# Products of constants in the waits that a kernel's own planner foresees for TensorE

## The chip, the core and the metric

The kernel runs on one core of a Trainium2 chip. The metric is the device time of one execution in microseconds (us), the median of three runs: 2536.06 us for the kernel before (2533.53 to 2548.08). Smaller is better.

## What is computed

One layer of a decoder trunk on 2048 tokens of width 1024, in fp32. The reference, cut to its frame:

```python
h = rms_norm(x, mix_norm_g)
qa, ka, va, pb, qm = split_cols(h @ w_in, ...)          # one combined projection
out_a = sliding_window_attention(q, k, va, sinks, rel_bias)      # 6 heads, window 128
out_b = rwkv7_mixer(token_shift(pb, mu), ...)           # 6 heads, a recurrent scan
out_m = memory_attention(qm, mk, mv)                    # 4 heads, 256 memory tokens
x = x + concat([out_a, out_b, out_m]) @ w_out
x = x + conv_ffn(rms_norm(x, ffn_norm_g), w_up, conv_w, conv_b, w_down)   # d_ff 2816
```

## The kernel before

The kernel is recorded first and written out afterwards. Each call on an engine goes into a `Recorder`, which notes an operation with its tiles, a duration from the function `cost` (L374) and what it depends on. `Recorder.order` (L229) and `run` (L257) then lay all operations out on a modelled time axis, engine by engine: when an engine is free, the ready operation with the longest modelled path behind it starts. Each operation `o` thereby has a modelled `o.start` and `o.end`. `Recorder.emit` (L330) writes the real instructions in that order; semaphores for the dependencies are added behind it. Beyond setting the order, the modelled times are used for nothing. All instructions are written by one line of `emit`, L345, so every row of the profile has L345, and groups are told apart by their tiles.

The work in order of time, by the profile:

- 0 to some 960 us: the input projection (tile `mm`: 4 blocks of 512 tokens x 17 column groups, each 8 x 3 products of 512 columns, since each fp32 operand is split into a high and a low fp32r part) with its post-processing (`st`, `bc`, `tpv`: transposes by the constant identity `ident`, a part of the tile `cst`), the RWKV scan (`pz`, `pc`, `pg`, `p1`, `px`, `pq`, `pu`, `pS`), and from 435 us on the window attention (`pl`, `tpa`, `po`) and the memory attention (`plm`, `tpm`, `pm`).
- to 1236 us: the output projection (`outproj`, L1271), four blocks of 512 tokens, the first two beside attention and scan. At the end of each block come the sums of squares of the new x: `st2` (the profile writes `st`), four fp32 products of a 128x128 tile `ss` with one column of ones, each into one column of a PSUM tile. From them follow `s` (VectorE), `r` (GpSimd), `tpr` (a TensorE transpose), `rt` (ScalarE), and the DMA to `drs`, on SyncE's queue.
- to the end: the feed-forward network in seven products for eight (`seven`, L1380; tiles `uf`, `uch`, `uip`), first `ffn_up` for both halves of the tokens, then `ffn_down`. It takes weights from DMA (`wraw`), split by ScalarE (`whi`) and VectorE (`wlo`).

PSUM is held in rings: tag `mm` has one buffer (used by `mm`, by `st2` and by `tpr`), so has `po`; `f`, `ch` and `ip` have two. A new tile of a ring waits until the last reader of the tile that held the buffer is done. A product with `start=True` overwrites what its PSUM tile held.

Of the kernel before, what the change touches and what calls it, by code (L numbers as in the profile page):

```python
# [18 lines left out]
P = 128  # L19
# [34 lines left out]
class View:  # L54
# [42 lines left out]
    def real(self):  # L97
        r = self.t.made()
        for f, a, k in self.path:
            r = bass.AP(r.tensor, r.offset + a[0], a[1]) if f == "ap" else getattr(r, f)(*a, **k)  # L100
        return r
# [28 lines left out]
class Recorder:  # L130
# [126 lines left out]
    def run(self):  # L257
# [69 lines left out]
        assert len(out) == len(ops)  # L327
        return out

    def emit(self, tc):  # L330
        nc, open_ = tc.nc, {}
        real = lambda v: v.real() if isinstance(v, View) else v
        out = self.out = self.order()
        with tc.manual_schedule():
            for o in out:
                if o.eng is None:
                    p = o.a[0]
                    if o.fn == "open":
                        kw = {k: v for k, v in (("space", p.space), ("side", p.side)) if v is not None}
                        open_[p] = tc.tile_pool(name=p.name, bufs=p.bufs, reuse_waits="tile", **kw)  # L340
                        p.obj = open_[p].__enter__()
                    else:
                        open_.pop(p).__exit__(None, None, None)
                else:
                    getattr(getattr(nc, o.eng), o.fn)(*map(real, o.a), **{k: real(v) for k, v in o.k.items()})  # L345
        return open_

# [59 lines left out]
class K:  # L407
# [5 lines left out]
    def consts(self):  # L413
        nc, tc, a = self.nc, self.tc, self.a
        p = self.rec.pool("const", 1)
        self.cp = p
        c = p.tile([P, CSTW], F32, name="cst")
        nc.sync.dma_start(out=c[:, 0:P], in_=a["cst"][:, 0:P])
        nc.sync.dma_start(out=c[:, P:], in_=a["cst"][:, P:])
        self.c = {n: c[:, o:o + w] for n, (o, w) in CST.items()}  # L420
        pp = p.tile([P, PPW], F32, name="pp")
        nc.sync.dma_start(out=pp, in_=a["pp"])
        self.pp = {n: pp[:, o:o + w] for n, (o, w) in PPC.items()}
        self.ident = self.c["ident"]
        self.mh = self.cp.tile([P, 10], F32, name="mh")
        nc.vector.memset(self.mh, -0.5)
        self.one = self.cp.tile([P, 1], F32, name="one")
        nc.vector.memset(self.one, 1.0)
# [1272 lines left out]
```

## Time and profile before

| | before |
|---|---|
| median of 3 runs | 2536.06 us (2533.53 to 2548.08) |
| the profiled execution | 2532.01 us |
| its span | 2530.1 us |
| mean granted TensorE clock | 0.966 of full |
| TensorE (PE) busy | 2403.9 us, 95% of the span |
| VectorE (DVE) busy | 2037.7 us, 81% |
| ScalarE (ACT) busy | 1256.3 us, 50% |
| DMA engines, mean busy share | 49.1% of 16 engines' span on the main queue |

The span is the time from the first to the last instruction; 1.9 us of the profiled execution lie around it. PE stands for the products on TensorE and PEld for its weight loads, which overlap the product before. A plain fp32 product is carried out as two passes, each with a weight load of its own: it stands in the program once and in the profile twice. Products of fp32r operands and transposes are one pass. In the profile's rows, `128*64 128x384` means a stationary operand of 128 rows and 64 columns and a moving operand of 384 columns. "Granted clock" 1.00 is 2.4 GHz, 0.50 is 1.2 GHz.

### The profile page before, as it was taken

To read this page: it belongs to the slowest core of one execution; us is meant where nothing else is said; L and a number is where in the kernel's file an instruction comes from. 1 tells how busy PE (TensorE), PEld (TensorE's weight loads), DVE (VectorE), ACT (ScalarE), POOL (GpSimd) and SP (SyncE) were. 2 spreads that over 40 slices of the span, in tenths; PEclk is the share of its full clock that TensorE was granted. 3 is DMA by queue.
4 is the path that set the end of the run, shared out by engine and by line. 5 is a ranking of instruction groups with operands and counts; after the bars stand their busy time and mean duration, and the time that the engine had idled before them with its cause. 6 is when DMAs were issued, how large, how long until landed. Compare 5 with 4: busy or idle time off the path is not lost.

```text
span 2530.1 us, 36859 instructions
## 1 busy us (share of the span) xinstructions
PE 2403.9 (95%) x12268; PEld 1897.1 (75%) x12268; DVE 2037.7 (81%) x4901; ACT 1256.3 (50%) x2541; POOL 78.5 (3%) x53
## 2 busy tenths in 40 slices
PE   8898999899898989999899999999999998999999
PEld 6777777666676757667788788888888886887887
DVE  6677778778778777769688998899888888878876
ACT  5354544555445554555354455565545463444442
POOL 1111011010000010000000000000000000000000
PEclk9999999989989989999999999999999998999999
DMA  7675745744344464547323733353233256548543
GB/s 230 192 214 153 212 131 149 203 138 121 114 134 124 128 183 137 177 134 259 109 97 111 265 130 106 111 179 137 99 108 106 88 166 205 166 150 274 157 146 111
DMA packets 292935, 389.32 MB, mean 154 GB/s; under 512 B 49911, under 2 KB 155392, under 8 KB 292744
## 3 DMA queue, kind: packets, MB, share of 16 engines
q1 hardware_dynamic: 292744, 386.96, 49.1%
q8 instruction: 97, 1.59, 0.3%
q14 instruction: 94, 0.77, 0.1%
HBM read 274.89 MB, written 111.97 MB: 153 GB/s over the span
## 4 chain that ended last, share of the span: by engine, by line
PE 77%; DVE 9%; DMA 6%; issue 4%; ACT 3%; SPq 0%; POOL 0%; POOLq 0%; DVEq 0%; ACTq 0%
PE uf L345 27%; PE mm L345 15%; PE uch L345 13%; PE uip L345 6%; PE pq L345 4%; DMA nb<-nbd 3%; PE pg L345 2%; PE po L345 2%; DMA wraw<-w_ip_in 2%; DVE wlo L345 1%; DVE uc L345 1%; PE pl L345 1%; PE tpa L345 1%; DVE h2l L345 1%; PE pu L345 1%
## 5 line engine op out<-in xcount | busy, mean ns | idle before, releaser
L345 ACT CAST whi<-wraw 128x512 fp32r<-128x512 f32 (+1 forms) x410 | 250.3, 613 | 367.8 <-PE mm L345 135.2
L345 PE MATMUL uf<-h2h,wlo 128*128 128x512 f32 x1056 | 412.4, 392 | 14.1 <-DVE wlo L345 14.1
L345 PE MATMUL uf<-h2h,whi 128*128 128x512 f32 x1056 | 413.9, 392 | 8.5 <-ACT whi L345 6.0
L345 PE MATMUL uf<-h2l,whi 128*128 128x512 f32 x1056 | 413.0, 391 | 0.0
L345 DVE TENSOR_TENSOR wlo<-wraw,whi 128x512 fp32r<-128x512 f32 (+1 forms) x410 | 277.3, 679 | 101.5 <-ACT whi L345 99.6
L345 ACT CAST whi<-ws 128x512 fp32r<-128x512 f32 (+1 forms) x272 | 164.8, 609 | 348.8 <-PE uf L345 163.7
L345 DVE SCALAR_TENSOR_TENSOR uc<-ub,pp,uc 128x1024 f32<-128x1024 f32 x176 | 225.0, 1282 | 26.2 <-ACT uc L345 25.2
L345 PE MATMUL mm<-hh,whi 128*128 128x512 f32 x544 | 226.7, 418 | 18.6 <-ACT whi L345 6.6
L345 PEld LDWEIGHTS uf<-h2h,wlo 128*128 128x128 f32 x1056 | 199.6, 189 | 57.0 <-DVE wlo L345 15.1
L345 PEld LDWEIGHTS uf<-h2h,whi 128*128 128x128 f32 x1056 | 199.4, 189 | 53.9 <-ACT whi L345 8.1
L345 PEld LDWEIGHTS uf<-h2l,whi 128*128 128x128 f32 x1056 | 199.6, 189 | 41.7 <-DVE h2l L345 0.7
L345 PE MATMUL mm<-hh,wlo 128*128 128x512 f32 x544 | 221.9, 409 | 1.4 <-DVE wlo L345 1.4
L345 PE MATMUL mm<-hl,whi 128*128 128x512 f32 x544 | 223.0, 410 | 0.0
L345 PE MATMUL uch<-h2h,whi 128*128 128x512 f32 x528 | 205.7, 390 | 0.1
L345 PE MATMUL uch<-h2h,wlo 128*128 128x512 f32 x528 | 205.8, 390 | 0.0
L345 PE MATMUL uch<-h2l,whi 128*128 128x512 f32 x528 | 205.5, 389 | 0.0
L345 DVE TENSOR_TENSOR wlo<-ws,whi 128x512 fp32r<-128x512 f32 (+1 forms) x272 | 181.3, 672 | 23.3 <-ACT whi L345 22.0
L345 PEld LDWEIGHTS mm<-hh,whi 128*128 128x128 f32 x544 | 105.9, 195 | 47.1 <-ACT whi L345 8.8
L345 ACT CAST h2h<-tr 128x512 fp32r<-128x512 f32 x182 | 110.3, 620 | 58.5 <-DMA tr<-dg 35.4
L345 DVE TENSOR_TENSOR xtmp<-xinv,nb 96x60 f32<-96x60 f32 (+24 forms) x496 | 100.7, 203 | 38.7 <-DMA nb<-nbd 34.5
L345 DVE TENSOR_TENSOR h2l<-tr,h2h 128x512 fp32r<-128x512 f32 x182 | 120.3, 688 | 9.2 <-ACT h2h L345 9.1
L345 ACT ACTIVATE uc<-ub,pp 128x1024 f32<-128x1024 f32 x88 | 109.7, 1247 | 34.0 <-DVE ub L345 32.9
(366 smaller groups left out, 4721.5 us busy)
## 6 DMA issues: line engine op xcount, KB each, us to landing
wraw<-w_up_in SPq DMA_DIRECT2D x176, 256.0 KB
tr<-dg SPq DMA_DIRECT2D x154, 256.0 KB
wraw<-w_ip_in SPq DMA_DIRECT2D x136, 256.0 KB
dg<-uc SPq DMA_DIRECT2D x88, 256.0 KB
dg<-tt SPq DMA_DIRECT2D x66, 256.0 KB
wraw<-w_op_in SPq DMA_DIRECT2D x64, 256.0 KB
wraw<-w_down_in SPq DMA_DIRECT2D x64, 256.0 KB
xk<-xT_in SPq DMA_DIRECT2D x56, 256.0 KB
```

The lines of the kernel that those rows point to most:

```text
L345: getattr(getattr(nc, o.eng), o.fn)(*map(real, o.a), **{k: real(v) for k, v in o.k.items()})
```

## The change

Where `emit` comes to a TensorE operation that starts a new group (a transpose, or a product with `start=True`), it now looks at the modelled wait ahead of it, `o.start` less the modelled end of TensorE's operation before. For each such wait it writes a number of products of the identity with itself first, into the tile that the operation is going to overwrite. Nothing reads them. They begin after the first transpose of the program.

```diff
+    def spin(self, nc, o, gap):
+        v = o.a[0]
+        (p0, p1), (c0, c1) = v.box
+        n = min(c1 - c0, P)
+        t = v.t.made()[p0:p1, c0:c0 + n]
+        a, b = self.warm.real()[:, 0:p1 - p0], self.warm.real()[:, 0:n]
+        for _ in range(int(min(gap, 2500) * 0.8 / (n / 0.6 + 4))):
+            nc.tensor.matmul(t, a, b, start=True, stop=True, skip_group_check=True)
...
+        last, seen = 0.0, False
...
+                    if o.eng == "tensor":
+                        if seen and (o.fn == "transpose" or o.k["start"]):
+                            self.spin(nc, o, o.start - last)
+                        seen = seen or o.fn == "transpose"
+                        last = o.end
                     getattr(getattr(nc, o.eng), o.fn)(*map(real, o.a), **{k: real(v) for k, v in o.k.items()})
...
-        self.ident = self.c["ident"]
+        self.ident = self.rec.warm = self.c["ident"]
```

The moving operand of such a product is as wide as the operation's own box in the PSUM tile, at most 128 columns (`n`); the stationary one has as many columns as the box has partitions. The count is 80% of the modelled wait, which is cut at 2500 ns, over `n / 0.6 + 4` ns for one product: 217.3 ns at 128 columns, 5.67 ns at one.

In the program this makes 743 products in 103 places, all ahead of 1405 us of the profile's time: 312 in 100 places, of which 238 have 128 stationary columns, 61 have 64 and 13 have 4; and 431 in three places with one moving and 128 stationary columns, all of them ahead of the sums of squares, since the box of `st[:, t:t + 1]` is one column wide: 28 in the output projection's first block, 54 in the second and 349 in the fourth. The order on VectorE, ScalarE, GpSimd and SyncE is as before, and so is TensorE's but for the new products.

A new product needs its PSUM buffer, but none of the operation's operands. So it takes over that part of the operation's wait that was for the buffer, if there was one, and the rest stays with the operation. By the two programs' waits, the operation keeps a wait of its own in 57 of the 100 places, and in 43 the new products carry the whole of it.

TensorE, where the fourth block's output projection ends and the feed-forward network begins, before (`st` are the sums of squares):

```order
L345 MATMUL mm<-ch,whi 128x512
L345 MATMUL mm<-cl,whi 128x512
L345 MATMUL mm<-ch,wlo 128x512
L345 MATMUL st_13849<-one,ss 128x1 x4
L345 MATMUL tpr<-cst,r 4x128
L345 MATMUL uf<-h2h_13087,whi 128x512
L345 MATMUL uf<-h2l_13153,whi 128x512
```

And the same place now (L338 is the line of the new products, `cst` their operand, L361 is what was L345):

```order
L361 MATMUL mm<-ch,whi 128x512
L361 MATMUL mm<-cl,whi 128x512
L361 MATMUL mm<-ch,wlo 128x512
L338 MATMUL st_14220<-cst 128x1 x349
L361 MATMUL st_14220<-one,ss 128x1 x4
L338 MATMUL tpr<-cst 4x128 x5
L361 MATMUL tpr<-cst,r 4x128
L338 MATMUL uf<-cst 128x128 x9
L361 MATMUL uf<-h2h_13450,whi 128x512
L361 MATMUL uf<-h2l_13516,whi 128x512
```

Three groups of new products stand between the last projection and the first product of the feed-forward network; nothing changed places.

TensorE at the sums of squares of the second block, among attention, before:

```order
L345 MATMUL po<-pt,va 64x384 x2
L345 MATMUL tpa<-cst,lg 128x128 x6
L345 MATMUL st_12921<-one,ss 128x1 x3
L345 MATMUL plm<-km,dq 128x256 x4
L345 MATMUL po<-pt,va 64x384 x2
```

And now:

```order
L338 MATMUL po<-cst 64x128 x5
L361 MATMUL po<-pt,va 64x384 x2
L338 MATMUL tpa<-cst 128x128 x2
L361 MATMUL tpa<-cst,lg 128x128 x6
L338 MATMUL st_13224<-cst 128x1 x54
L361 MATMUL st_13224<-one,ss 128x1 x3
L361 MATMUL plm<-km,dq 128x256 x4
L361 MATMUL po<-pt,va 64x384 x2
```

Wide and narrow products alternate with the work; the attention's `plm` and `po` now stand behind the 54 narrow ones.

## Rows read from the trace of the kernel before

**Rows 1.** The page's busy times, its chain, and the answer on the clock.
```profile
PE 2403.9 (95%) x12268; PEld 1897.1 (75%) x12268; DVE 2037.7 (81%) x4901; ACT 1256.3 (50%) x2541; POOL 78.5 (3%) x53
...
PE 77%; DVE 9%; DMA 6%; issue 4%; ACT 3%; SPq 0%; POOL 0%; POOLq 0%; DVEq 0%; ACTq 0%
...
core 0: 2530.1 us, clock 0.966
```

**Rows 2.** Timeline, weight loads of the sums of squares: start us, us, instructions.
```profile
1015.97 0.98 PEld L345 LDWEIGHTS st<-one,ss 128*128 128x128 f32 x8
...
1232.20 0.98 PEld L345 LDWEIGHTS st<-one,ss 128*128 128x128 f32 x4
```

**Rows 3.** The page's costliest groups, weight loads: busy us, mean ns, idle before.
```profile
L345 PEld LDWEIGHTS uf<-h2l,whi 128*128 128x128 f32 x1056 | 199.6, 189 | 41.7 <-DVE h2l L345 0.7
```

**Rows 4.** Timeline of PE, 1229 to 1243 us; brackets: idle before and its releaser.
```profile
1229.11 0.39 PE L345 MATMUL mm<-ch,wlo 128*128 128x512 f32 x1
1231.73 1.54 PE L345 MATMUL st<-one,ss 128*128 128x1 f32 x8 [2.23 <-DVE ss L345]
1234.68 0.37 PE L345 MATMUL tpr<-cst,r 128*4 128x128 f32 x1 [1.41 <-POOL r L345]
1239.03 0.80 PE L345 MATMUL uf<-h2h,whi 128*128 128x512 f32 x1 [3.98 <-ACT whi L345]
1239.62 0.63 PE L345 MATMUL uf<-h2l,whi 128*128 128x512 f32 x1
...
1242.18 0.48 PE L345 MATMUL uf<-h2l,whi 128*128 128x512 f32 x1
```

**Rows 5.** Timeline of DVE in the same place.
```profile
1229.54 0.69 DVE L345 TENSOR_TENSOR xk<-mm,xk 128x512 f32<-128x512 f32 x1 [3.30 <-PE mm L345]
1230.98 0.69 DVE L345 TENSOR_TENSOR ss<-ss,sq 128x512 f32<-128x512 f32 x1 [0.75 <-ACT sq L345]
```

**Rows 6.** Stretches: us, busy PE, PEld, DVE, ACT, POOL (instructions), clock, DMA share, GB/s.
```profile
696.23:713.30 17.07, 16.85 (x73) 12.03 (x74) 9.92 (x44) 7.25 (x22) 0.00 (x0) 0.50 0.53 147
720.12:726.95 6.83, 6.83 (x36) 5.94 (x35) 4.92 (x14) 2.61 (x9) 0.00 (x0) 0.50 0.23 66
1300.00:1400.00 100.00, 99.53 (x440) 82.04 (x438) 83.67 (x123) 51.09 (x73) 0.00 (x0) 1.00 0.31 103
```

**Rows 7.** Timeline of PE at the second block's sums of squares.
```profile
1123.35 0.73 PE L345 MATMUL st<-one,ss 128*128 128x1 f32 x6
1124.03 0.74 PE L345 MATMUL plm<-km,dq 128*128 128x256 f32 x4
```

**Rows 8.** Timeline of PE behind the first block's sums of squares.
```profile
1016.09 0.94 PE L345 MATMUL st<-one,ss 128*128 128x1 f32 x8
...
1026.76 0.49 PE L345 MATMUL mm<-ch,whi 128*128 128x512 f32 x1 [2.30 <-ACT ch L345]
1027.73 0.80 PE L345 MATMUL mm<-cl,whi 128*128 128x512 f32 x1 [0.47 <-DVE cl L345]
```

**Rows 9.** Timeline, weight loads of 128 and of 64 columns.
```profile
1014.28 0.64 PEld L345 LDWEIGHTS tpb<-cst,bk 128*128 128x128 f32 x6
...
1017.25 0.42 PEld L345 LDWEIGHTS pm<-ptm,vm 128*64 128x64 f32 x8 [0.31 <-ACT ptm L345]
```

**Rows 10.** Timeline of PE: first and last place where the operation keeps its wait.
```profile
18.66 0.43 PE L345 MATMUL tps<-cst,ms 128*128 128x128 f32 x2 [0.57 <-POOL ms L345]
...
1401.57 0.50 PE L345 MATMUL uf<-h2h,whi 128*128 128x512 f32 x1 [2.04 <-ACT whi L345]
```

**Rows 11.** Timeline of PE: first and last idle place where the new products carry it.
```profile
19.55 0.55 PE L345 MATMUL tp<-cst,xt 128*128 128x128 f32 x3 [0.46 <-ACT xb L345]
...
934.98 0.79 PE L345 MATMUL mm<-ch,whi 128*128 128x512 f32 x1 [0.78 <-DVE xk L345]
```

**Rows 12.** Stretches at half the clock beside new wide products: first and last of ten, sum.
```profile
105.73:109.14 3.41, 3.41 (x10) 2.63 (x9) 1.73 (x6) 0.00 (x0) 2.34 (x2) 0.50 0.93 301
...
1402.79:1409.62 6.83, 4.96 (x12) 3.90 (x13) 6.83 (x13) 1.29 (x3) 0.00 (x0) 0.50 0.94 286
...
sum 78.51, PE 62.76 PEld 42.36 DVE 61.52 ACT 32.85 POOL 7.97; mean PE 6.28 PEld 4.24 DVE 6.15 ACT 3.29 POOL 0.80
```

## The prediction

> **What bounds the kernel now.** I read the page's busy times and its chain first [rows 1]. TensorE is busy for 2403.9 of 2530.1 us and holds 77% of the chain; it stands idle for 126 us in all. So whatever is added to TensorE's queue where it does not wait lengthens the kernel, and even where it waits there is little room: 743 products that cost more than these 126 us cannot be hidden in any arrangement. The second thing to see is the clock: a mean of 0.966 at levels 1.00 and 0.50 means that (1 - 0.966) / 0.5 = 6.8% of the span, 172 us, went by at half clock. That is what products in the waits could win back. The third is what one product costs, and here the timeline of the sums of squares matters most, since 431 of the 743 products have that shape.
>
> **The narrow products, price.** The four products of `st` are eight passes in the profile, and their eight weight loads take 0.98 us from the first's start to the last's end [rows 2]. A load takes 0.19 us [rows 3], so the loads start (0.98 - 0.19) / 7 = 0.113 us apart: one moving column or not, a pass costs its weight load. A narrow product costs 0.226 us at full clock, against the 5.67 ns by which it was counted out, forty times as much. At half clock 0.98 us holds four loads, not eight; with a load 1.7 steps long, as at full clock, a step is 0.98 / 4.7 = 0.209 us. The 512-column products agree in ratio: 0.427 us apart at half clock ((1242.18 - 1239.62) / 6, [rows 4]), 100 / 440 = 0.227 at full [rows 6], a factor of 1.88. I take 0.113 x 1.88 = 0.213, or 0.426 us a product.
>
> The Trainium skill, "TensorE: Matmul & The Clock Gate", section "Wait — 56ns, not 53.3ns?", gives some 25 ns as the least from one product's start to the next, however narrow. By that the 862 passes of the 431 products would take 21.6 us (an estimate from that page). Here no row shows such a rate where each pass loads weights, so it stands among the rivals only.
>
> **Which clock they run at.** This is the large choice. Before, the last wide product ends at 1229.50 us, and by 1232.20 the loads already run at half clock [rows 2, 4]. A busy TensorE alone does not hold the clock: for 17 us from 696 on it was busy 16.85 of 17.07 us at 0.50, and from 720 on 6.83 of 6.83 us at 0.50, both in stretches with many small passes of the scan; the stretch from 1300 on, equally busy with 512-column products, is at 1.00 throughout [rows 6]. A narrow run streams one column a pass, less than any of these. So I let the clock fall some 4 us into each run (2 to 10) and stay low until wide products come. The trace has no run of narrow products over 1.5 us; both levels are therefore bounds.
>
> **(a) The 349 in the fourth block.** Their PSUM buffer is that of the last `mm`, which `xk` on VectorE reads until 1230.23 [rows 5]. So they start near 1230.3, while the operation behind them was ready at 1231.73. 18 products at full clock take 4.0 us, 331 at half 141.0; they end at 1375.3, and `st` starts 143.6 us late. The wait of 2.23 us hides 1.4 us of this, no more. Who waits for it: `s`, `r`, `tpr`, `rt`, the DMA to `drs` on SyncE's queue and behind that the first weights `wraw` of the feed-forward network, so the whole chain moves by that amount. No other engine has work in that place that could be pulled forward, and what follows is bound by TensorE. The 5 products ahead of `tpr` and the 9 ahead of `uf` lie in waits of 1.41 and 3.98 us [rows 4] and change that by 1 us at most. Bounds: 135 to 147 for a fall of the clock after 10 or 2 us.
>
> **(b) The 54 in the second block.** There `st` follows the work before it without a wait, and `plm` follows at 1124.03 [rows 7], so nothing hides them: 4.0 us for 18 at full clock and 36 x 0.426 = 15.3 at half, 19.3 us (12.2 if the clock holds, 21 if it falls sooner).
>
> **(c) The 28 in the first block.** Also without a wait [rows 8]: 4.0 + 10 x 0.426 = 8.3 us. Ten us further on TensorE waited 2.30 and 0.47 us for `ch` and `cl`, which do not hang on these sums; that takes up 2.8 us. 5.5 remain (3.5 to 9). In (b) and (c) the `drs` DMA is late by the same time and SyncE's queue holds the scan's and the weights' loads behind it; they are late together with TensorE, so I add nothing, but it is why I let no more of the delay be absorbed.
>
> **(d) After (b) and (c)** the clock needs wide products to rise; 3.4 us at half clock each cost 3.4 x 0.47 = 1.6 us, 3 together (0 to 4). After (a) it was low before, too.
>
> **(e) The 312 others.** Six loads of 128 columns take 0.64 us and eight of 64 columns 0.42 us [rows 9], so a product is some 0.226 us with 128 stationary columns and 0.105 with 64 or fewer: 238 x 0.226 + 74 x 0.105 = 61.6 us. I laid each of the 100 places beside its operation in the trace. In the 57 that keep a wait of their own (the first and the last in [rows 10]) 37.7 us of products meet 43.5 us of idle time, badly matched: 11.2 us stick out, mostly where the planner foresaw a wait and none came. In the other 43 [rows 11] the products first wait for the buffer as the operation did, and all their 23.9 us come on top. That is 35 us if nothing gives way behind them. Half of it should: a late TensorE finds VectorE and ScalarE, busy 81% and 50%, further ahead at the next wait. I take 18 (5 to 40, the upper end with some of them at half clock).
>
> **(f) The clock won back.** Ten half-clock stretches, 78.5 us, have groups of new wide products just ahead of or in them, and TensorE was busy for 62.8 us of them [rows 12]. All at full clock, 62.8 x 0.47 = 29 us. Some fall because of idle time that the products do not reach, so I take half, -15 (0 to -29).
>
> **Sum.** 143.6 + 19.3 + 5.5 + 3 + 18 - 15 = 174.4 us on the profiled execution's 2532.0, or 2706 us. That execution lies 4 us below the median of the runs and inside them; I leave this to scatter. With all bounds on one side, 2658 and 2753.
>
> **Rivals.** *The clock holds in the narrow runs.* For it: TensorE has no idle time in them. Against it: the stretches at 0.50 in [rows 6]. (a) then is 1230.3 + 78.9 - 1231.7 = 77.5, (b) 12.2, (c) 6.3 - 2.8 = 3.5; with (e) and (f) as above 96 us, so 2628 (2597 to 2665). The Trainium skill's page named above asks, under "Why this matters for your kernels", that TensorE be kept busy without a break for its clock to stay up; by that sentence this rival is the right one, and the profile's stretches speak against it here.
>
> *The narrow passes are cheap*, since all have the same stationary operand and only the first would need its load. The place is the run of 349. At the counted 5.67 ns the 431 take 2.4 us, all hidden, and 18 - 15 leaves 2535: not slower. The point from which it decides is 11 ns a pass (862 x 0.011 + 3 = 12.5 us, 0.5%). Against it: `uf<-h2l,whi` follows a product with the same weights `whi`, and the profile has a load of its own for each of the 1056 [rows 3]. At the page's 25 ns a pass it would be 2553.
>
> *The waits get the clock back.* If narrow passes are cheap and (e) and (f) stand at their good ends, 5 - 29 = -24: 2508, faster. It needs the rival before it, so it is the least likely.
>
> **How the numbers follow.** Chances: the forecast 0.78, the holding clock 0.13, cheap passes 0.04, faster 0.03; the remaining 0.02 lies in mixtures above 2550. About 0.5% is what a measurement of this kernel can tell from no change. So faster 0.03, within 0.04, slower 0.93. The forecast's own range, 2658 to 2753, holds about 0.67; to leave out no more than 0.2 the range must take in the holding clock as well, and I give 2600 to 2750.
>
> **What would show it.** In the trace after: a run of `st<-cst` of 698 passes near 1240 us, some 145 us long (79 if the clock holds), with VectorE, ScalarE and the DMA idle in it, clock 0.50 nearly throughout and loads 0.21 us apart. `st` first at 1375 us or later; the feed-forward part as long as before. 54 narrow products over 12 to 21 us near 1130, 28 over 6 to 9 near 1016. In the input projection the half-clock stretches of [rows 12] partly gone, the span up to 1016 within some 20 us of before. It is wrong if the 698 passes run closer than 0.1 us, if the clock holds, or if the wide products cost over 40 us.

## The result, and the profile after

The changed kernel takes 2702.1 us, the median of four runs (2697.8 to 2706.77), against 2540.39 us for the kernel before in the same set: 1.0648 of it, interval 1.062 to 1.0676, slower. The prediction said 2706, with 2600 to 2750 as its range. The profiled execution took 2706.77 us with a span of 2705.0 us; the one before had 2532.01 us, so 174.8 us lie between the two traces.

The page of the kernel after, busy times and the chain, and the answer on the clock; they answer to [rows 1]:

```profile
PE 2621.7 (97%) x13754; PEld 2127.2 (79%) x13754; DVE 2038.7 (75%) x4901; ACT 1257.0 (46%) x2541; POOL 77.2 (3%) x53
...
PE 81%; DVE 8%; DMA 6%; ACT 2%; issue 2%; SPq 0%; DVEq 0%; POOL 0%; ACTq 0%
...
core 0: 2705.0 us, clock 0.950
```

The other engines do the same work in the same time; TensorE has 1486 more passes, 2 x 743, and is busy 217.8 us longer. It is idle for 83 us, against 126: the products took 43 us of idle time away and 175 us came on top.

The timeline of TensorE at the three runs of narrow products, in order of time. `st<-cst` are the new products, `st<-one,ss` the sums of squares:

```profile
1019.71 8.22 PE L338 MATMUL st<-cst 128*128 128x1 f32 x56
1027.79 1.85 PE L361 MATMUL st<-one,ss 128*128 128x1 f32 x8
...
1133.12 20.01 PE L338 MATMUL st<-cst 128*128 128x1 f32 x108
1152.99 1.42 PE L361 MATMUL st<-one,ss 128*128 128x1 f32 x6
...
1261.90 145.22 PE L338 MATMUL st<-cst 128*128 128x1 f32 x698 [0.78 <-DVE xk L361]
1406.99 1.84 PE L361 MATMUL st<-one,ss 128*128 128x1 f32 x8
1409.16 2.30 PE L338 MATMUL tpr<-cst 128*4 128x128 f32 x10 [0.33 <-DVE s L361]
...
1415.65 0.50 PE L361 MATMUL uf<-h2h,whi 128*128 128x512 f32 x1 [1.28 <-ACT whi L361]
```

The run of 349 products is one row of 698 passes and 145.22 us. Its bracket names `xk` on VectorE, the reader of the PSUM buffer: from then on nothing is waited for. What the engines did in it, and which clock TensorE had, is seen in stretches (columns as in [rows 6]):

```profile
1262.00:1266.00 4.00, 4.00 (x37) 4.00 (x37) 0.69 (x1) 0.57 (x1) 0.00 (x0) 1.00 0.17 66
1266.14:1406.90 140.76, 140.76 (x662) 140.76 (x661) 0.00 (x0) 0.00 (x0) 0.00 (x0) 0.50 0.00 1
```

TensorE and its weight loads are busy without a gap, VectorE, ScalarE and the DMA engines do nothing, and after 4.2 us the clock goes to half and stays there. A pass takes 140.76 / 661 = 0.213 us. The two shorter runs go the same way: from 1023.79 and from 1136.43 on, 4.1 and 3.3 us after their first pass, the granted clock is 0.50:

```profile
1023.79:1034.03 10.24, 10.24 (x52) 9.81 (x53) 2.49 (x10) 0.26 (x1) 1.12 (x1) 0.50 0.43 109
1136.43:1160.33 23.90, 23.90 (x105) 21.66 (x106) 2.13 (x5) 1.45 (x4) 0.56 (x1) 0.50 0.09 29
```

### The profile page after: what moved, and what is told of

Its sections match the earlier page's. It is cut to its first block, busy times and chain, and to the rows that moved or that the text cites. A ratio compares the mean times of both kernels' runs of the same rounds, so it can differ in the third digit from the quotient of the medians.

```text
span 2705.0 us, 39822 instructions
## 1 busy us (share of the span) xinstructions
PE 2621.7 (97%) x13754; PEld 2127.2 (79%) x13754; DVE 2038.7 (75%) x4901; ACT 1257.0 (46%) x2541; POOL 77.2 (3%) x53
## 4 chain that ended last, share of the span: by engine, by line
PE 81%; DVE 8%; DMA 6%; ACT 2%; issue 2%; SPq 0%; DVEq 0%; POOL 0%; ACTq 0%
PE uf L361 25%; PE mm L361 15%; PE uch L361 12%; PE st L338 6%; PE uip L361 6%; PE pq L361 4%; DMA nb<-nbd 2%; PE pg L361 2%; PE po L361 2%; DVE wlo L361 1%; PE pl L361 1%; DVE uc L361 1%; PE st L361 1%; DVE h2l L361 1%; PE tpa L361 1%
## 5 line engine op out<-in xcount | busy, mean ns | idle before, releaser
L361 PE MATMUL uf<-h2h,wlo 128*128 128x512 f32 x1056 | 411.9, 391 | 14.6 <-DVE wlo L361 14.6
L361 ACT CAST whi<-wraw 128x512 fp32r<-128x512 f32 (+1 forms) x410 | 250.7, 614 | 367.6 <-PE mm L361 137.5
L361 PE MATMUL uf<-h2h,whi 128*128 128x512 f32 x1056 | 412.7, 391 | 2.2 <-ACT whi L361 1.3
L361 PE MATMUL uf<-h2l,whi 128*128 128x512 f32 x1056 | 412.3, 391 | 0.0
L361 DVE TENSOR_TENSOR wlo<-wraw,whi 128x512 fp32r<-128x512 f32 (+1 forms) x410 | 277.1, 679 | 94.2 <-ACT whi L361 90.7
L361 ACT CAST whi<-ws 128x512 fp32r<-128x512 f32 (+1 forms) x272 | 164.7, 609 | 350.1 <-PE uf L361 163.9
L361 PEld LDWEIGHTS uf<-h2h,wlo 128*128 128x128 f32 x1056 | 199.1, 189 | 58.1 <-DVE wlo L361 16.6
L361 DVE SCALAR_TENSOR_TENSOR uc<-ub,pp,uc 128x1024 f32<-128x1024 f32 x176 | 225.0, 1282 | 26.1 <-ACT uc L361 25.2
L361 PEld LDWEIGHTS uf<-h2h,whi 128*128 128x128 f32 x1056 | 199.0, 188 | 46.3 <-ACT whi L361 3.7
L361 PEld LDWEIGHTS uf<-h2l,whi 128*128 128x128 f32 x1056 | 198.9, 188 | 42.0 <-DVE h2l L361 0.9
L361 PE MATMUL mm<-hh,whi 128*128 128x512 f32 x544 | 222.4, 410 | 5.9 <-ACT whi L361 3.9
L361 PE MATMUL mm<-hh,wlo 128*128 128x512 f32 x544 | 218.2, 402 | 1.4 <-DVE wlo L361 1.3
L361 PE MATMUL mm<-hl,whi 128*128 128x512 f32 x544 | 218.8, 402 | 0.1
L361 PE MATMUL uch<-h2h,whi 128*128 128x512 f32 x528 | 205.6, 389 | 0.2 <-ACT whi L361 0.2
L361 PE MATMUL uch<-h2l,whi 128*128 128x512 f32 x528 | 205.6, 389 | 0.0
L361 PE MATMUL uch<-h2h,wlo 128*128 128x512 f32 x528 | 205.5, 389 | 0.0
L361 DVE TENSOR_TENSOR wlo<-ws,whi 128x512 fp32r<-128x512 f32 (+1 forms) x272 | 181.2, 672 | 23.6 <-ACT whi L361 22.4
L338 PE MATMUL st<-cst 128*128 128x1 f32 (+1 forms) x922 | 181.7, 335 | 0.8 <-DVE xk L361 0.8
L338 PEld LDWEIGHTS st<-cst 128*128 128x128 f32 x922 | 181.1, 308 | 1.2 <-DVE xk L361 1.2
L361 ACT CAST h2h<-tr 128x512 fp32r<-128x512 f32 x182 | 110.3, 620 | 55.6 <-DMA tr<-dg 35.3
L361 DVE TENSOR_TENSOR xtmp<-xinv,nb 96x60 f32<-96x60 f32 (+24 forms) x496 | 100.8, 203 | 36.5 <-DMA nb<-nbd 32.3
L361 PEld LDWEIGHTS mm<-hh,whi 128*128 128x128 f32 x544 | 103.5, 191 | 30.6 <-ACT whi L361 5.0
```

Of the source, the lines that this page charges most:

```text
L338: nc.tensor.matmul(t, a, b, start=True, stop=True, skip_group_check=True)
```

## The experiments

My theory: the narrow products cost their weight loads, at half clock because one moving column a pass does not hold it, and nothing hides them; the wide ones cost little on balance. The rivals: products of constants do not hold the clock whatever their width, a pass has a fixed price, or the wide ones are what costs. Each experiment changes the new function `spin` or the condition that calls it. Ratios are to the kernel before on the same chip.

**Without the narrow products.**

```diff
-                        if seen and (o.fn == "transpose" or o.k["start"]):
+                        if seen and (o.fn == "transpose" or o.k["start"]) and o.a[0].shape[-1] > 1:
```

> Leaves out the 431 products with one moving column and keeps the 312 others. Theory of the prediction: cost (e) of about 18 us and clock won back (f) of about 15 us cancel; in the trace after, the first products of the sums of squares came 3.6 us later than before and the part behind them lost nothing, so 3 to 6 us above the kernel before, within 0.5%. Rival 'wide products cost in full' (35 us, nothing given back by the clock): 1.4% slower. Rival 'the clock won back outweighs them': 15 us or more faster.

2531.45 us, 0.9975 (0.9955 to 0.9994), 4.3 us faster than the 2535.72 of before by the medians. So on balance the 312 wide products do not cost anything, and the 431 narrow ones are the whole loss: 170.7 us by the difference of the two ratios, (1.0648 - 0.9975) x 2537, and 166 by the medians. The small rest has the other sign than expected, which had been read from one pair of traces; it lies between the theory and the rival of a clock that pays back 15 us.

**Narrow products made 128 columns wide.** Same number, same places, same stationary operand.

```diff
-        t = v.t.made()[p0:p1, c0:c0 + n]
-        a, b = self.warm.real()[:, 0:p1 - p0], self.warm.real()[:, 0:n]
+        w = P if n == 1 else n
+        t = v.t.made()[p0:p1, c0:c0 + w]
+        a, b = self.warm.real()[:, 0:p1 - p0], self.warm.real()[:, 0:w]
```

> All 743 products in the same places and numbers, but the 431 stream 128 columns of the identity in place of one. A pass is paced by its weight load either way, so at the same clock the time would not change. Theory (one column a pass does not hold the clock): the clock stays at 1.00 in the run of 349, which lasts 349 x 0.226 = 79 us, and the kernel is some 65 to 75 us faster than the change, 92 to 100 us above the kernel before. Rival 'products of constants don't hold the clock, whatever their width': half clock as in the change, 160 us or more above the kernel before.

2618.52 us, 1.0333 (1.0303 to 1.0364): some 80 us faster than the change by the two ratios, though these products stream 128 times as many columns, and 83 us above the kernel before. That is 9 to 17 us better than the theory's numbers, of which 7 to 10 us are the wide rest, which gives 4 us where 3 to 6 us of cost were expected, and nothing like the rival's 160. The timeline of TensorE and the stretch of the run of 349:

```profile
1245.94 78.21 PE L339 MATMUL st<-cst 128*128 128x128 f32 x698 [0.79 <-DVE xk L362]
...
1246.00:1324.00 78.00, 78.00 (x699) 78.00 (x700) 0.69 (x1) 0.61 (x1) 0.00 (x0) 1.00 0.01 4
```

The clock stays at 1.00 throughout, over the two shorter runs as well, and a pass takes 78.21 / 698 = 0.112 us, as one narrow pass did at full clock in [rows 2]. Both operands are still the identity. So the width of what is streamed decided about the clock, not the constants, and not whether TensorE was busy: it was busy without a gap in both kernels. Where between one and 128 columns this turns, no run shows.

**Narrow products with 64 stationary columns.**

```diff
         n = min(c1 - c0, P)
+        p1 = p0 + 64 if n == 1 else p1
```

> As the change, but the 431 narrow products have 64 stationary columns in place of 128 (and write 64 partitions). Theory (a narrow pass costs its weight load, and the clock stays at half): a pass takes half as long, 0.107 us; the run of 349 some 74 us in place of 145, all narrow runs together some 80 us less, so about 2620 us. Rival 'a pass has a fixed price whatever it loads': 2702 us as the change.

2613.38 us, 1.0301 (1.0267 to 1.0334), near the 2620 expected:

```profile
1239.83 73.62 PE L339 MATMUL st<-cst 128*64 128x1 f32 x698 [0.78 <-DVE xk L362]
...
1241.00:1313.00 72.00, 72.00 (x679) 72.00 (x678) 0.22 (x1) 0.00 (x0) 0.00 (x0) 0.50 0.01 3
```

Half the stationary columns, half the time: 72.00 / 678 = 0.106 us a pass at the same half clock. The price is that of the weight load. All passes of a run have the same stationary operand, and every one loads it again.

**Only the places in which the operation keeps a wait of its own.** The 57 are listed by their number in TensorE's order; 202 wide products.

```diff
+                        at += 1
-                        if seen and (o.fn == "transpose" or o.k["start"]):
+                        if at in places and seen and (o.fn == "transpose" or o.k["start"]):
```

> Only the 57 places in which the operation behind keeps a wait of its own (202 wide products; no narrow ones). Theory: 11 us stick out, half of it absorbed, and most of the clock won back hangs on these places: 5 to 20 us faster than the kernel before. Rival 'idle time is worth nothing, the clock pays nothing back': 0 to 11 us slower.

2522.39 us, 0.9946 (0.9927 to 0.9964), 13.3 us faster than before, inside the 5 to 20 expected: products that run while the operand is still awaited do pay.

**Only the other 43 places**, by the same edit; 110 wide products.

> Only the 43 places in which the products take over the operation's whole wait (110 wide products; no narrow ones). Theory: 23.9 us of products on TensorE's path, half absorbed behind them, little clock: 5 to 15 us slower than the kernel before. Rival 'they are hidden or paid back by the clock as well as the others': within 5 us.

2541.58 us, 1.0023 (1.0009 to 1.0036), 5.9 us slower, in the theory's range; the interval, 2 to 9 us, takes in the rival's 5 as well, and the next experiment decides between them. The two together make -7.4 us, close to the -4.3 of all 312.

**The 43 places with twice the products.**

```diff
-        for _ in range(int(min(gap, 2500) * 0.8 / (n / 0.6 + 4))):
+        for _ in range(2 * int(min(gap, 2500) * 0.8 / (n / 0.6 + 4))):
```

> The 43 places in which the products take over the operation's whole wait, with twice the number of products: 220 in place of 110, 24 us more on TensorE's path. Theory (about half is absorbed behind them, and the clock has little more to give): 10 to 15 us slower than with 110, that is 15 to 21 us slower than the kernel before. Rival 'they are absorbed or paid back by the clock': within 8 us of the kernel before.

2562.51 us, 1.0098 (1.0075 to 1.0122), 25.3 us slower than before and 19.4 us slower than with 110 products. So 19.4 of the added 24 us come through, four fifths (some 12 to 26 us with the two intervals taken together), where 10 to 15 were expected, and the rival is out. The granted clock of its profiled execution is 0.968, no better than with 110 (0.973). What is added behind a wait for the buffer is for the most part paid.

**A version by measured waits.** The planner's waits replaced by those of the trace of before: 40 places in which TensorE stood idle for over 0.35 us ahead of an operation that starts a group and keeps a wait of its own, each filled to 90% at the measured price, with at least 128 columns in place of one.

```diff
-        n = min(c1 - c0, P)
+        n = P if c1 - c0 == 1 else min(c1 - c0, P)
-        for _ in range(int(min(gap, 2500) * 0.8 / (n / 0.6 + 4))):
+        for _ in range(int(gap * 0.9 / (max(n, p1 - p0) / 0.6 + 10))):
...
+                        self.spin(nc, o, waits.get(at, 0))
```

> Products of the identity, at least 128 columns wide where the operation's box is one column, in 40 places where the trace of the kernel before has over 0.35 us of idle time ahead of an operation that starts a group and keeps a wait of its own; 90% of the measured idle time over the measured price (0.226 us at 128 columns): 220 products. Theory (idle time that is really there, filled at its real length, gives the clock back at no cost): better than the 57 places by the planner's waits, 15 to 25 us faster than the kernel before. Rival 'waits shift from execution to execution and a filled one moves the next': no better than those, 10 to 15 us faster.

2517.93 us, 0.992 (0.990 to 0.994), 19.3 us faster than before, inside the 15 to 25 expected, and faster than both kernels. That it is better than the 57 places by the planner's waits (0.9946) is likely but not shown: the two intervals overlap, and the two versions differ in the choice and number of their places as well (40 with 220 products, 57 with 202). The clearest place is the one where the kernel before waited 5.17 us for `sq`. Its timeline of TensorE before, then in this version:

```profile
229.70 0.39 PE L345 MATMUL pc<-cst,sg 128*128 128x130 f32 x2
235.26 1.94 PE L345 MATMUL st<-cst,sq 128*128 128x128 f32 x8 [5.17 <-DVE sq L345]
...
238.74 0.63 PE L345 MATMUL mm<-hl,whi 128*128 128x512 f32 x1
```

```profile
228.79 4.63 PE L338 MATMUL st<-cst 128*128 128x128 f32 x40
233.75 1.31 PE L360 MATMUL st<-cst,sq 128*128 128x128 f32 x8 [0.33 <-DVE sq L360]
...
235.95 0.39 PE L360 MATMUL mm<-hl,whi 128*128 128x512 f32 x1
```

The 20 products fill the wait but for 0.33 us, and what follows runs at full clock: the projection's products last 0.39 us each where they lasted 0.63. Over the part up to 1016 us the granted clock is 0.97 in this version (the second row) against 0.94 before (the first):

```profile
0.00:1016.00 1016.00, 933.46 (x5635) 698.64 (x5636) 774.94 (x2743) 515.32 (x1306) 73.12 (x49) 0.94 0.55 161
```

```profile
0.00:1016.00 1016.00, 960.77 (x6028) 730.24 (x6029) 787.74 (x2793) 521.36 (x1319) 74.53 (x50) 0.97 0.56 164
```

The changed kernel has the same clock in this part:

```profile
0.00:1016.00 1016.00, 960.90 (x6116) 739.82 (x6117) 772.12 (x2731) 513.62 (x1299) 72.34 (x49) 0.97 0.56 160
```

But the operation that the kernel before starts at 1016 us comes 3.6 us later there, ahead of the narrow products, and 17.0 us earlier in this version. So by these traces the version by measured waits does not hold the clock better than the change; it pays less for it.

## Why the prediction was right, step by step

I laid the same operations of the two traces beside each other and read how late each came.

- **Price of a narrow pass**: 0.213 us at half clock as taken from [rows 2, 4, 6], 0.112 at full. Right, and the experiment with 64 stationary columns shows the reason.
- **The clock in the runs**: it fell 3.3 to 4.2 us into each of the three, against "some 4 us", a choice that no row of before gave. Right; the run of 349, busy for 140.76 of 140.76 us at 0.50, rules out the rival that the clock holds because TensorE is busy, and the experiment with 128 columns shows that the width makes the difference. The Trainium skill's page "TensorE: Matmul & The Clock Gate", under "Why this matters for your kernels", asks that TensorE be kept busy without breaks. Read as a promise for any kind of work, that does not hold in these traces.
- **(a)** The sums of squares of the fourth block came 175.26 us late (1231.73 before, 1406.99 after), the product ahead of the run 31.62: 143.6 us, the figure predicted. (Its bounds of 135 and 147 do not come out: by its own prices a clock that falls after 10 or 2 us gives 138 and 146. That moves the forecast's own low end, 2658, up by some 3 us and leaves the stated range as it is.) All of it stayed: `uf` started 176.6 us late (1239.03 to 1415.65) and the last one 174.9.
- **(b)** 19.9 us between the last `tpa` and the first `st` in the second block (9.8 us late, then 29.6), 19.3 predicted.
- **(c)** 8.1 us in the first block, 8.3 predicted. The waits for `ch` and `cl` of [rows 8] are gone from the trace after, as expected, and 6.4 us remain (5.5 predicted, and 1.6 of clock under **(d)**). Behind the second block's run the lateness grows by another 2.0 us to the 31.62, wide products included, against 1.6 under **(d)**.
- **(e) and (f)** together are where the terms were mis-sized, in opposite ways. Their sum up to the first run was 3.6 us in the traces (3 predicted) and -4.3 us by the medians without the narrow products. But the cost is higher: what is carried behind a wait for the buffer comes through to four fifths, not to half, so some 28 of the 35 us (an estimate from the two experiments on the 43 places, and as uncertain as they are). And the clock gives back more. The median granted clock is 0.9815 over the twelve runs without the narrow products and 0.965 over the 25 of the kernel before beside them, so half clock took (1 - 0.9815) / 0.5 x 2530 = 94 us in place of (1 - 0.965) / 0.5 x 2534 = 177: 83 us less, where I had counted on about half of 78.5. With the busy share and the factor of **(f)**, 83 x 0.8 x 0.47 = 31 us were won back, not 15. That is an estimate, but it fits: 28 of cost and -4.3 in all want 32.
- **Rivals.** Cheap passes by a stationary operand that is already there: no, each pass has its load. The waits get the clock back: right as a mechanism, as the 57 places and the version by measured waits show, but not in this change. The clock that holds: no, as said; its low end by its own terms is 2601 and not 2597.

One price in **(e)** was wrong. For the 36 products with 64 or 4 stationary columns and 128 moving ones I took 0.105 us. The timeline of TensorE after has ten such passes in a row, at full clock:

```profile
1129.12 1.31 PE L338 MATMUL po<-cst 128*64 128x128 f32 x10
```

In the trace's single records those behind the first start 0.109 us apart, so such a product costs 0.22 us: the wider of the two operands sets the pace. It adds about 4 us to the products' sum.

The mechanism was right, and the narrow products' terms (a) to (d) add up to 171.4 us, where the experiments give 166 to 171. That the whole sum agrees to 0.4 us between the two profiled executions (174.8 against 174.4) is luck. By the medians it was 162 us: the profiled execution after was the slowest of its four, and the one before was faster than all of its four. More than half of the difference is **(e)** and **(f)**, forecast at 3 us in all and measured at -4.3.

## What to carry to other kernels

Price a filler product by the passes that it really is: two for plain fp32, each at the pace of the wider of its stationary and moving operands (0.112 us at 128 columns and full clock here). A formula in the moving width alone was out by a factor of 40 and cost some 170 us. Products without use paid here where TensorE really stood idle for an operand (13.3 us faster), and cost where it stood idle for the buffer that the product itself must wait for (5.9 us slower). A long run of them should stream wide. Take the idle time from a trace: the traced waits gave 19 us; the planner's, where they were waits for an operand, gave 13, though the two are not clearly apart.

## What the runs showed of the hardware

That the clock goes to half under a TensorE that is busy for 140.76 of 140.76 us was expected; that 128 identity columns a pass hold it at full for 78 us, with an operand that is zero but for its diagonal, was open. The width gave back as much as the experiment expected: 128 columns in place of one made the same 698 passes 67 us shorter.
